# Three weight tiles of the first projection in two float32r parts, their low parts made on GpSimd

## The chip, the cores and the metric

The kernel runs on one core of one Trainium2 chip. The metric is the device time of one execution in microseconds (us). Engines are named as the profile names them: PE (TensorE matmul) with PEld (its weight loads), DVE (VectorE), ACT (ScalarE), POOL (GpSimd) and SP (SyncE, whose queue issues the transfers).

## What is computed

Two transformer-like blocks on 256 tokens of width 1024, in float32. Only the start of the first block bears on the change: one wide input projection, cut into parts, of which the first two feed a gated causal convolution 31 taps wide.

```python
h = x @ w_in[l] + b_in[l]
conv_a, conv_g, q, k, v, r, f_lr, gate_a, gate_b = jnp.split(h, split_points, axis=-1)
...
u = a * jax.nn.sigmoid(g)                       # a, g: conv_a, conv_g
u = conv(u, conv_w, width 31, causal, per channel) + conv_b
u = jax.nn.silu(layer_norm(u, ln_g, ln_b))
return u @ w_co + b_co
```

The rest of block 1 is a gated linear attention branch on `q, k, v, r, f_lr`, an output projection, a layer norm and a mixture of 64 experts; block 2 follows. The expert weights are most of the 527 MB that are read.

## The kernel before

Weights arrive as tiles of 128 x 2048 float32 (1 MB), one after the other in a fixed order, `W[0]`, `W[1]`, ...; the ring that holds them has four buffers. The first eight tiles are the projections `a` and `g` in turn: tile 0 is a0, tile 1 g0, tile 2 a1, tile 3 g1, tile 4 a2, tile 5 g2, tile 6 a3, tile 7 g3. Tiles 8 and 9 are `k`, then come `q`, `r`, `v`, the gates and the output projections. `proj_T` multiplies a tile in one of two ways:

- **Split.** `split` makes two float32r tiles: ACT casts the high part `hi` (L295; three buffers, `hlh`), DVE subtracts it from the weight for the low part `lo` (L297; two buffers, `hll`). PE then runs, for each half of the tile, 16 matmuls on `hi` (L343 with the high part of the input, L344 with its low part) and 8 on `lo` (L346): 48 per tile.
- **Whole.** With the tile's number in `WHOLE`, PE multiplies the float32 tile by the float32 input `xt` (L334), 16 matmuls per tile, each two records in the trace. ACT and DVE have nothing to do for it, and `xt` keeps a buffer of the weight ring until the last whole tile.

`proj_tok` (tiles 8, 9 and later) multiplies the other way round, with L362, L363 and L366 for the same three kinds.

Beside the projections run tasks that `pump` deals out at fixed places of the program. `fg` holds the decay of the attention branch (PE L490, then exponential and logarithm on ACT L492 and L495, then DVE L497, then PE L502, ...), `bg` the taps of the convolution. When a `g` tile is finished, `ev_g` computes sigmoid on ACT (L535) and the product `u` on DVE (L536, which reads PSUM), and queues 62 taps: two on ACT (L525), 60 on DVE (L527, `acc = u*w + acc`, all operands in SBUF). Four such groups make 240 taps on DVE. Behind the last tap DVE adds up the channels (L781), PE finishes that sum (L785), DVE subtracts the mean (L791) and adds up the squares (L794), PE finishes them (L799), and so on: the layer norm of the convolution, whose PE steps stand at fixed places between the projections of the later tiles. DVE also runs L692 (the scaled residual, `x1`) and L661 (a gate product) in that stretch.

A scheduler orders each engine's instructions when the program is built; on the chip each engine runs its own list in that order. The names of the change: `WHOLE`, `split`, `proj_T`, `nc.vector`, `nc.gpsimd`. POOL has nothing to do in the kernel before but a few powers on 1 to 8 columns (`rpow`, L379, and L1250).

Of the kernel before, what the change touches and what calls it, by code (L numbers as in the profile page):

```python
# [9 lines left out]
F32 = mybir.dt.float32  # L10
# [4 lines left out]
ALU = mybir.AluOpType  # L15
# [16 lines left out]
Z_MIN = 8  # L32
N_RING = (4, 1, 5)
E_BIAS, N_BIAS = 20, 7
WHOLE = (0, 5, 6, 7)

# [160 lines left out]
class Builder:  # L199
    def __init__(self, tc, I, ctx):  # L200
# [4 lines left out]
        self.after, self.ready, self.held = None, [], []  # L205
        self.whole = WHOLE
        pool = lambda **k: ctx.enter_context(tc.tile_pool(**k))
# [78 lines left out]
    def split(self, src, shape, pool, tag="hl"):  # L286
        nc = self.nc
        hi = self.t(pool, shape, tag + "h", F32R, bufs=3)
        lo = self.t(pool, shape, tag + "l", F32R, bufs=2)
        n = 2 if self.wi == 1 else 1  # L290
        late = lambda i: self.tc.issue_after(self.after[i].ins) if self.after is not None else ExitStack()
        for i in range(n):
            ks = slice(i * shape[1] // n, (i + 1) * shape[1] // n)
            with late(0):
                nc.scalar.copy(hi[:, ks], src[:, ks])  # L295
            with late(1):
                nc.vector.tensor_tensor(lo[:, ks], src[:, ks], hi[:, ks].bitcast(F32), ALU.subtract)  # L297
        self.pump(self.npump)
        return hi, lo

# [1432 lines left out]
```

## Time and profile before

| | |
|---|---|
| median of 3 runs | 1705.51 us (1702.78 to 1706.95) |
| the profiled execution, time | 1704.66 us |
| its span in the trace | 1702.9 us |
| PE busy / PEld busy | 87% / 68% |
| DVE busy / ACT busy / POOL busy | 44% / 31% / 1% |
| mean granted TensorE clock | 0.89 of full speed |

A share of the whole span says little here: the first 290 us (block 1 up to the experts) are matmuls with much DVE work, the next 850 us are the experts with the transfers at some 418 GB/s, and the rest is block 2. What the change touches lies between 30 and 70 us. A timeline row gives the start, the time from the first start to the last end of the merged instructions, engine, line, operation, output and inputs, shapes and the count; in brackets stands idle time just before it and what ended that. PE ends are modelled, so a tile's cost is best read from start to start.

### The profile page before, as it was taken

The page shows a single profiled execution, that of the slowest core. Times are in us where ns is not written, and L with a number is a line of the kernel's source. Part 1 is how long each engine was busy: PE and PEld are TensorE (multiplying, and loading weights), DVE is VectorE, ACT ScalarE, POOL GpSimd, SP SyncE. Part 2 cuts the span into 40 slices and gives each one's busy share as a digit, 9 for nine tenths or more (in the row PEclk, how much of TensorE's full clock was granted, in tenths as well). Part 3 has the DMA queues.
Part 4 walks back from the last instruction along what each step waited for, and adds up shares of the span by engine and source line. Part 5 has one row for each costly group of instructions (what it writes and reads, how often), then busy time and mean ns, then how long its engine had stood idle before and what let it go on. Part 6 is the DMA issues. An engine that isn't in the chain of part 4 may idle for free. (4 is left out here: it accounts for less than half of the span.)

```text
span 1702.9 us, 34326 instructions
## 1 busy us (share of the span) xinstructions
PE 1486.3 (87%) x14632; PEld 1154.9 (68%) x14632; DVE 749.8 (44%) x1487; ACT 527.4 (31%) x916; POOL 16.1 (1%) x22
## 2 busy tenths in 40 slices
PE   8999998877766787788888878868799999999998
PEld 7898996544444454455565545534699998899986
DVE  6999975311111121111121112211676866666645
ACT  4554552211111011111011111101585554555433
POOL 0000000000000000000000000000001000000000
PEclk9999999987788788887678788867899999999999
DMA  7555588999999999999999999999545444555551
GB/s 280 203 200 198 211 313 343 418 417 419 418 418 420 418 419 418 417 419 418 419 418 418 419 418 420 417 396 380 200 142 188 151 166 147 187 188 182 183 186 71
DMA packets 74516, 530.61 MB, mean 312 GB/s; under 512 B 8309, under 2 KB 8309, under 8 KB 11000
## 3 DMA queue, kind: packets, MB, share of 16 engines
q1 hardware_dynamic: 74354, 528.36, 78.1%
q8 instruction: 117, 1.92, 0.5%
q14 instruction: 39, 0.32, 0.1%
q10 hardware_dynamic: 6, 0.01, 0.0%
HBM read 527.29 MB, written 1.05 MB: 310 GB/s over the span
## 5 line engine op out<-in xcount | busy, mean ns | idle before, releaser
L966 PE MATMUL ps<-w,xg 128*32 128x256 f32 x4032 | 304.6, 449 | 74.0 <-DMA w<-in_wm_dram 71.6
L297 DVE TENSOR_TENSOR hll<-w,hlh 128x2048 fp32r<-128x2048 f32 (+1 forms) x112 | 252.5, 2256 | 96.3 <-PE ps L346 53.6
L966 PEld LDWEIGHTS ps<-w,xg 128*32 128x32 f32 x4032 | 131.6, 125 | 221.5 <-DMA w<-in_wm_dram 114.1
L295 ACT CAST hlh<-w 128x2048 fp32r<-128x2048 f32 (+1 forms) x112 | 210.6, 1881 | 164.0 <-PE ps L344 77.9
L343 PE MATMUL ps<-s,hlh 128*128 128x256 f32 x864 | 216.6, 289 | 1.0 <-ACT hlh L295 0.8
L344 PE MATMUL ps<-s,hlh 128*128 128x256 f32 x864 | 212.3, 283 | 0.3 <-DVE s L1284 0.2
L983 PE MATMUL ps<-w,hT 128*32 128x128 f32 x4032 | 167.9, 326 | 49.7 <-DMA w<-in_wm_dram 23.3
L972 DVE TENSOR_TENSOR h<-h,ps 64x256 f32<-64x256 f32 x63 | 26.6, 423 | 375.9 <-ACT h L971 375.9
L983 PEld LDWEIGHTS ps<-w,hT 128*32 128x32 f32 x4032 | 136.7, 131 | 69.5 <-DVE hT L977 23.7
L343 PEld LDWEIGHTS ps<-s,hlh 128*128 128x128 f32 x864 | 165.0, 191 | 4.5 <-issue 2.2
L344 PEld LDWEIGHTS ps<-s,hlh 128*128 128x128 f32 x864 | 165.5, 192 | 1.3 <-DVE s L318 0.6
L971 ACT ACTIVATE h<-ps 64x256 f32<-64x256 f32 x63 | 23.8, 378 | 406.1 <-PE ps L966 397.1
L987 DVE COPY ys<-ps 32x128 f32<-32x128 f32 x240 | 68.2, 284 | 155.4 <-PE ps L983 153.7
L987 ACT COPY ys<-ps 32x128 f32<-32x128 f32 x240 | 61.9, 258 | 236.3 <-PE ps L983 232.5
L346 PE MATMUL ps<-s,hll 128*128 128x256 f32 x864 | 121.3, 283 | 0.3 <-DVE hll L297 0.3
L346 PEld LDWEIGHTS ps<-s,hll 128*128 128x128 f32 x864 | 111.4, 192 | 0.5 <-DVE hll L297 0.5
L527 DVE SCALAR_TENSOR_TENSOR w<-w,vec,w 128x255 f32<-128x255 f32 (+14 forms) x240 | 94.3, 464 | 0.0
L1237 PEld LDWEIGHTS ps<-rel,con 32*128 32x128 f32 x512 | 82.2, 246 | 9.9 <-issue 7.6
L343 PE MATMUL ps<-w,hlh 128*128 128x256 f32 x352 | 86.1, 283 | 0.0
L1237 PE MATMUL ps<-rel,con 32*128 32x8 f32 x512 | 85.6, 298 | 0.0
L344 PE MATMUL ps<-w,hlh 128*128 128x256 f32 x352 | 84.8, 279 | 0.0
L995 PE MATMUL ps<-ys,WT 128*128 128x512 f32 x120 | 79.1, 816 | 0.0
(390 smaller groups left out, 1764.3 us busy)
## 6 DMA issues: line engine op xcount, KB each, us to landing
w<-in_wm_dram SPq DMA_DIRECT2D x378, 1024.0 KB, 19.8
w<-in_w_dram SPq DMA_DIRECT2D x115, 1024.0 KB, 4.8
gain<-in_row_dram SPq DMA_DIRECT2D x4, 512.0 KB, 5.0
w<-in_wpp_dram SPq DMA_DIRECT2D x2, 768.0 KB
w<-in_xT_dram SPq DMA_DIRECT2D x2, 512.0 KB, 5.5
w<-in_w_dram SPq DMA_DIRECT2D x2, 512.0 KB
x<-in_x_dram SPq DMA_DIRECT2D x1, 1024.0 KB
w<-in_wab_dram SPq DMA_DIRECT2D x1, 1024.0 KB, 5.3
```

The lines of the kernel that those rows point to most:

```text
L295: nc.scalar.copy(hi[:, ks], src[:, ks])
L297: nc.vector.tensor_tensor(lo[:, ks], src[:, ks], hi[:, ks].bitcast(F32), ALU.subtract)
L343: nc.tensor.matmul(o, hi[:, k, ms], xh[:, k, :], start=(k == 0), stop=False)
L344: nc.tensor.matmul(o, hi[:, k, ms], xl[:, k, :], start=False, stop=False)
L346: nc.tensor.matmul(o, lo[:, k, ms], xh[:, k, :], start=False, stop=(k == 7))
L527: nc.vector.scalar_tensor_tensor(a, u[:, m, :T - d], wj, a, ALU.mult, ALU.add)
L966: r = nc.tensor.matmul(pa[j * 32:(j + 1) * 32, :256], xg[:, k, c0:c0 + CAP], w[:, j * 256:(j + 1) * 256], start=(k == 0), stop=(k == KC - ...
L972: nc.vector.tensor_tensor(h, h, pa[64:128, :256], ALU.mult)
L983: r = nc.tensor.matmul(py[j % 2][j * 32:(j + 1) * 32, :P], hT[:, k % 2, k // 2, :], w[:, j * P:(j + 1) * P], start=(k == 0), stop=(k == 3) ...
L987: eng(ys[r0:r0 + CAP, c * 512 + j * P:c * 512 + (j + 1) * P], py[j % 2][j * 32:(j + 1) * 32, :P])
L995: self.nc.tensor.matmul(self.acc[t][c], WT[:rows, t * P:(t + 1) * P], ys[:rows, c * 512:(c + 1) * 512], start=False, stop=True, skip_group ...
L1237: nc.tensor.matmul(ps[:, i * 8:(i + 1) * 8], self.con[0:32, o + x:o + x + P], rel, start=True, stop=True)
```

## The change

Tiles 5, 6 and 7 (g2, a3, g3) leave `WHOLE` and go through `split` like their neighbours. In `split` the number `self.wi` has already been raised, so `POOLED = (6, 7, 8)` names the same three tiles; for them the subtraction that makes `lo` is issued on POOL. `self.whole` is empty in block 2, so nothing goes to POOL there.

```diff
-WHOLE = (0, 5, 6, 7)
+WHOLE = (0,)
+POOLED = (6, 7, 8)
...
             with late(1):
-                nc.vector.tensor_tensor(lo[:, ks], src[:, ks], hi[:, ks].bitcast(F32), ALU.subtract)
+                eng = nc.gpsimd if self.whole and self.wi in POOLED else nc.vector
+                eng.tensor_tensor(lo[:, ks], src[:, ks], hi[:, ks].bitcast(F32), ALU.subtract)
```

The scheduler's order changes with it. Line numbers of the changed kernel are one higher from L36 on and two higher behind the second hunk (L295 becomes L296, L297 L299, L527 L529, L781 L783, L794 L796).

POOL, from its first instruction of the program on. First the kernel before, then the changed one (`rs` and `crs` are outputs of powers):

```order
L379 ISA
L379 TENSOR_TENSOR rs_126_1320<-rp_1321,mhalf 128x4
L379 TENSOR_TENSOR rs_159_1584<-rp_1585,mhalf 128x4
L379 TENSOR_TENSOR crs_1985<-rp_1986,mhalf 128x1
L379 TENSOR_TENSOR crs_1990<-rp_1991,mhalf 128x1
```

```order
L299 ISA
L299 TENSOR_TENSOR hll_415<-w_412,hlh_414 128x2048
L299 TENSOR_TENSOR hll_483<-w_480,hlh_482 128x2048
L299 TENSOR_TENSOR hll_553<-w_550,hlh_552 128x2048
L381 TENSOR_TENSOR rs_132_1428<-rp_1429,mhalf 128x4
L381 TENSOR_TENSOR rs_165_1692<-rp_1693,mhalf 128x4
```

Three subtractions on 2048 columns, for tiles 5, 6 and 7, now stand ahead of the powers.

ACT, from the cast of tile 4 (`hlh_351` in both) up to the table of the logarithm; `e_344` is the sigmoid of tile 3, `e_439` and `e_475` that of tile 5, `ps_447` and its like the decay. Before, then changed:

```order
L295 CAST hlh_351<-w_349 128x2048
L535 ACTIVATE e_344<-ps_291,vec 128x256 x2
L525 ACTIVATE w_129<-w_128,vec 128x256 x2
L535 ACTIVATE e_439<-ps_412,vec 128x256 x2
L491 ACTIVATE w_126<-ps_447 128x512
L525 ACTIVATE w_129<-w_128,vec 128x256
L491 ACTIVATE w_126<-ps_450 128x512
L525 ACTIVATE w_129<-w_128,vec 128x256
L492 ACT_TABLE_LOAD
L492 ACTIVATE w_126<-w_126 128x1024
L295 CAST hlh_520<-w_518 128x2048
L495 ACT_TABLE_LOAD
```

```order
L296 CAST hlh_414<-w_412 128x2048
L296 CAST hlh_482<-w_480 128x2048
L537 ACTIVATE e_344<-ps_291,vec 128x256 x2
L527 ACTIVATE w_129<-w_128,vec 128x256 x2
L296 CAST hlh_552<-w_550 128x2048
L296 CAST hlh_628<-w_626 128x2048
L537 ACTIVATE e_475<-ps_422,vec 128x256 x2
L493 ACTIVATE w_126<-ps_486 128x512
L493 ACTIVATE w_126<-ps_489 128x512
L527 ACTIVATE w_129<-w_128,vec 128x256
L494 ACT_TABLE_LOAD
L494 ACTIVATE w_126<-w_126 128x1024
```

The casts of tiles 5 and 6 now stand ahead of the sigmoid of tile 3, and those of tiles 7 and 8 ahead of the sigmoid of tile 5.

DVE, around the last taps and the layer norm of the convolution (`hll` is the low part of a later tile, `x` the residual). Before, then changed:

```order
L527 SCALAR_TENSOR_TENSOR w_129<-w_128,vec,w_129 128x226
L692 SCALAR_TENSOR_TENSOR x_71<-x_71,gain 128x1024
L781 TENSOR_REDUCE e_1879<-w_129 128x256
L297 TENSOR_TENSOR hll_1885<-w_1882,hlh_1884 128x2048
L692 SCALAR_TENSOR_TENSOR x_71<-x_71,gain 128x1024
L297 TENSOR_TENSOR hll_1950<-w_1947,hlh_1949 128x2048
L791 TENSOR_TENSOR w_129<-w_129,mean_1877 128x1024 x2
L794 TENSOR_REDUCE e_1879<-w_1919 128x256
L794 TENSOR_REDUCE e_1880<-w_1919 128x256
L661 SCALAR_TENSOR_TENSOR w_1181<-w_1181,ps_1893 128x512
```

```order
L529 SCALAR_TENSOR_TENSOR w_129<-w_128,vec,w_129 128x226 x2
L299 TENSOR_TENSOR hll_1993<-w_1990,hlh_1992 128x2048
L783 TENSOR_REDUCE e_1987<-w_129 128x256
L299 TENSOR_TENSOR hll_2058<-w_2055,hlh_2057 128x2048
L793 TENSOR_TENSOR w_129<-w_129,mean_1985 128x1024 x2
L694 SCALAR_TENSOR_TENSOR x_71<-x_71,gain 128x1024
L796 TENSOR_REDUCE e_1987<-w_2027 128x256
L663 SCALAR_TENSOR_TENSOR w_1289<-w_1289,ps_2001 128x512
L796 TENSOR_REDUCE e_1988<-w_2027 128x256
```

Ahead of the second L794 stand the same low parts and all 240 taps in both; one L692 has gone behind it, and one L661 has come ahead of it. On PE the steps L785 and L799 stand between the same matmuls as before.

## Rows read from the trace of the kernel before

**Rows 1.** Windows of 10 us: busy us (count) per engine, PE clock, DMA share, GB/s
```profile
40.00:50.00 10.00, 10.00 (x48) 8.16 (x47) 10.00 (x27) 2.03 (x5) 0.00 (x0) 1.00 0.12 22
...
180.00:190.00 10.00, 10.00 (x87) 10.00 (x86) 10.00 (x11) 5.50 (x8) 0.00 (x0) 1.00 0.43 147
...
200.00:210.00 10.00, 8.10 (x53) 7.87 (x53) 8.10 (x11) 4.62 (x4) 1.07 (x2) 0.83 0.78 300
...
300.00:310.00 10.00, 8.61 (x194) 6.34 (x190) 5.84 (x27) 2.00 (x8) 0.00 (x0) 0.88 1.02 419
```

**Rows 2.** Timeline of PE around the whole tiles (columns told above)
```profile
35.16 0.28 PE L343 MATMUL ps<-w,hlh 128*128 128x256 f32 x1
...
40.81 7.07 PE L334 MATMUL ps<-w,w 128*128 128x256 f32 x32
47.71 1.88 PE L490 MATMUL ps<-gup,mean 128*128 128x512 f32 x4
49.43 13.98 PE L334 MATMUL ps<-w,w 128*128 128x256 f32 x64
```

**Rows 3.** Timeline of DVE, layer norm of the convolution
```profile
185.66 1.22 DVE L692 SCALAR_TENSOR_TENSOR x<-x,gain 128x1024 f32<-128x1024 f32 x1
186.79 3.86 DVE L781 TENSOR_REDUCE e<-w 128x256 f32<-128x2048 f32 x1
...
198.45 3.88 DVE L794 TENSOR_REDUCE e<-w 128x256 f32<-128x1024 f32 x2
202.24 0.68 DVE L661 SCALAR_TENSOR_TENSOR w<-w,ps 128x512 f32<-128x512 f32 x1
```

**Rows 4.** Timeline of PE, same stretch
```profile
190.79 0.67 PE L785 MATMUL ps<-e,ones 128*128 128x256 f32 x2 [0.27 <-DVE e L781]
...
202.38 0.83 PE L799 MATMUL ps<-ones,e 128*128 128x1 f32 x6 [1.46 <-DVE e L794]
```

**Rows 5.** Timeline of DVE from tile 4's low part to the decay
```profile
32.51 2.28 DVE L297 TENSOR_TENSOR hll<-w,hlh 128x2048 fp32r<-128x2048 f32 x1
35.86 0.87 DVE L536 SCALAR_TENSOR_TENSOR w<-ps,vec,e 128x256 f32<-128x256 f32 x2 [1.08 <-ACT e L535]
36.66 11.86 DVE L527 SCALAR_TENSOR_TENSOR w<-w,vec,w 128x248 f32<-128x248 f32 x31
...
57.39 1.29 DVE L497 SCALAR_TENSOR_TENSOR w<-ps,w 128x512 f32<-128x512 f32 x2
...
72.59 2.29 DVE L297 TENSOR_TENSOR hll<-w,hlh 128x2048 fp32r<-128x2048 f32 x1 [1.21 <-issue]
```

**Rows 6.** Timeline of ACT, same stretch
```profile
35.35 0.84 ACT L535 ACTIVATE e<-ps,vec 128x256 f32<-128x256 f32 x2 [4.82 <-PE ps L346]
...
47.97 0.84 ACT L535 ACTIVATE e<-ps,vec 128x256 f32<-128x256 f32 x2 [10.50 <-PE ps L334]
...
53.11 1.88 ACT L295 CAST hlh<-w 128x2048 fp32r<-128x2048 f32 x1
...
56.30 1.06 ACT L495 ACTIVATE w<-w 128x1024 f32<-128x1024 f32 x1
```

**Rows 7.** POOL's L379 at 1277 to 1281 us: duration ns min/median/max, first and last start
```profile
L379 POOL TENSOR_TENSOR krs<-rp,mhalf x2: 697/1720/2743, 1277.5 to 1280.2; 128x2 f32<-128x2 f32 x2
```

**Rows 8.** Timeline of DVE, same stretch
```profile
1277.41 2.28 DVE L297 TENSOR_TENSOR hll<-w,hlh 128x2048 fp32r<-128x2048 f32 x1
```

**Rows 9.** Timeline of POOL, a power beside taps and one on a column
```profile
149.47 1.18 POOL L379 TENSOR_TENSOR rs<-rp,mhalf 128x4 f32<-128x4 f32 x1 [149.01 <-DVE rp L378]
...
268.13 0.54 POOL L379 TENSOR_TENSOR rs<-rp,mhalf 128x1 f32<-128x1 f32 x1 [61.80 <-DVE rp L378]
```

**Rows 10.** Timeline of DVE: the taps beside it, and an operation on one column
```profile
16.47 0.15 DVE L1417 TENSOR_TENSOR gk<-vec 128x1 f32<-128x1 f32 x1
...
149.31 2.39 DVE L527 SCALAR_TENSOR_TENSOR w<-w,vec,w 128x248 f32<-128x248 f32 x6
151.62 2.28 DVE L297 TENSOR_TENSOR hll<-w,hlh 128x2048 fp32r<-128x2048 f32 x1
```

## The prediction

> **What bounds the kernel now.** I read the windows first, then the timelines of PE and DVE in block 1, then the few rows in which POOL and DVE work side by side. Between 40 and 50 us PE is busy all the time and so is DVE, at full clock, while transfers move next to nothing (22 GB/s); at 180 to 190 us PE and DVE are still both full [rows 1]. So two engines run level through the first 200 us of block 1, and the question is which of them sets its end. The answer stands at the layer norm of the convolution. PE reaches L785 with 0.27 us to wait for DVE, and at L799 it waits 1.46 us for DVE's L794 [rows 4]. DVE has no such wait: L692, L781 and L794 stand in a queue that is full from behind [rows 3], and the only idle time that its timeline shows between L536 at 35.86 us and this place is the 1.21 us ahead of one low part [rows 5]. DVE's queue sets when PE may pass L799; PE is the one that waits. From 300 us on the transfers are saturated (419 GB/s, DMA share 1.02) [rows 1]. They are issued as buffers of block 1 come free, and their total is fixed, so I take a shift of block 1's end as a shift of the end of the kernel, one to one.
>
> **The change, part by part.** *PE.* A split tile takes 5.65 us from start to start (35.16 to 40.81), a whole one 6.90 us (40.81 to 47.71; the two later ones 13.98 / 2 = 6.99) [rows 2]. Three tiles save 3 x 1.25 = 3.75 us of PE. That is the whole of what the change can give, and by itself it would end at 1704.66 - 3.75 = 1700.9 us. But it makes PE come 3.75 us earlier to a place where it already waits for DVE.
>
> *DVE, what it has to do.* DVE never made a low part for these tiles, so the change takes nothing from it. By the order, ahead of the second L794 stand the same taps and the same number of low parts; one L692 (186.79 - 185.66 = 1.13 us to the next start [rows 3]) has gone behind, one L661 (some 0.6 us; its record is 0.68 [rows 3]) has come ahead: -0.5 us.
>
> *ACT, three more casts.* Each takes 1.88 us [rows 6]. The cast of tile 6 now stands ahead of tile 3's sigmoid. With three buffers for the high part it must wait until PE has done tile 3, which is when the sigmoid started before, at 35.35 us [rows 6]; so the sigmoid starts at 37.23, and DVE's L536, 0.51 us behind it in the rows (35.86 - 35.35) [rows 5, 6], at 37.74. It is 1.88 us later, with one tap (11.86 / 31 = 0.383 us [rows 5]) done ahead of it: DVE loses 1.5 us. The cast of tile 8 stands ahead of tile 5's sigmoid in the same way; that starts at 40.81 + 5.65 + 1.88 + 0.26 = 48.6 us (0.26 is the step from 47.71 [rows 2] to 47.97 [rows 6]). DVE gets there with L536's 0.80 us (36.66 - 35.86) and 28 taps at 37.74 + 0.80 + 10.72 = 49.3 us, so nothing is lost there.
>
> *The decay.* ACT needs from the start of that sigmoid to the end of the logarithm 57.36 - 47.97 = 9.39 us, one cast of 1.88 us included [rows 6], which the new order puts elsewhere: 48.6 + 7.5 = 56.1 us. DVE, with L536 and 13 taps behind 49.3, stands at L497 at 55.0 and waits 1.1 us, where it came just in time before (57.39 [rows 5] behind 57.36). Against this, the idle 1.21 us of rows 5 goes, since PE frees that buffer earlier. Without any contact between POOL and DVE the sum is -0.5 + 1.5 + 1.1 - 1.2 = **+0.9 us**: DVE ends a little later than before and PE's 3.75 us become waiting at L785 and L799. What a longer wait there does to the clock is small: after the wait at L799 the window has 0.83 of full speed, a mean of the levels of 1.2 and 2.4 GHz [rows 1], and that loss is paid today too.
>
> *POOL, three subtractions of 2048 columns.* No row shows one. From below: the same operation on DVE, 2.28 us [rows 8]. From above: on a single column, where hardly anything but the fixed cost counts, a POOL power takes 0.54 us [rows 9] and a DVE operation 0.15 us [rows 10], a ratio of 3.6, which would make 8.2 us. One row shares the operation, the other the engine; I take the geometric middle, Q = 4.3 us, and keep both ends. The Trainium skill's page "GPSIMD Engine Reference", § 3.1, gives 4497 ns for a two-input operation of this size; by it the sum below would be 0.6 us larger. If nothing else happened Q would be free: each low part is needed only 16 matmuls (5.65 / 3 = 1.9 us) into its tile. For tile 5 POOL starts when PE is done with tile 3 (two buffers), 35.35, and has until 42.7 us; for tile 6 it starts at 41.0 and has until 50.1 (tile 6 starts behind L490 at 46.46 + 1.72, the step from 47.71 to 49.43 [rows 2]). The weight loads that now wait on SP for POOL's read are tiles 9 to 11, wanted only after 60 us, and transfers are idle there.
>
> *POOL against DVE.* This is the term that decides. At 1277.41 DVE runs a low part, with both inputs in SBUF [rows 8]; the POOL power that starts 0.1 us later takes 2.74 us, where the same power right behind it, beside no such operation, takes 0.70 [rows 7]. 2.74 - 0.70 = 2.04 us is what is left of DVE's 2.28 us: POOL waited until DVE was done. So the two share a way into SBUF and the later one is held out. In the other direction one place speaks for less: beside a power on 4 columns of 1.18 us [rows 9] DVE ran six taps in 151.62 - 149.31 = 2.31 us, 0.385 each [rows 10], no slower than the 0.383 of rows 5. That power got in between two taps, and reads 4 columns; how long it held the way the row cannot tell. A subtraction reads 2 x 2048 columns over its whole length. The Trainium skill, page "SBUF — State Buffer", § Who interferes with whom, says more than these rows: whichever starts first has the shared ports for its whole instruction, and a DVE instruction with two SBUF inputs is among those that contend. By that rule each Q below counts in full; by the taps of rows 10 alone it would count nothing, and the sum would stay at +0.9 us.
>
> I take it in full. Taps have both tensors in SBUF. Tile 5's subtraction (35.35 to 39.65) meets DVE only from 38.54 on, when L536, which reads PSUM, is done: Q - 3.2 us. Tile 6's (from 41.0) and tile 7's (from 46.6, when tile 5's buffer is free) fall into the 28 taps: Q each. Together 3Q - 3.2 = 9.7 us. The wait at L497 shrinks from 1.1 to some 0.5 us, since ACT's chain contains a tap that waits for the late L536. **Sum: -0.5 + 1.5 + 0.5 - 1.2 + 9.7 = +10.0 us**, and 1704.66 + 10.0 = 1714.7 us. The profiled execution lies 0.85 us below the median of the runs shown, so a median would be 1715.5; I say **1715**. With Q = 2.28 tile 5's part is nothing and the sum is +4.9 (1709.6); with Q = 8.2 it is +21.7 (1726.4). PE would stand at L502 for the late decay and at L785, always for DVE.
>
> **The rivals.** *No holding out in this direction* (rows 10 for it, rows 7 and 8 against): +0.9 us, 1705.6. This is the one on the other side, not slower: it decides if POOL lets taps through while it reads.
>
> *PE's gain arrives:* 1700.9. For it speaks that every low part before the layer norm is ready in time; against it that DVE has no idle time to give and the same work ahead of L794. It needs DVE to end 3.75 us earlier out of nothing, or L799 not to wait.
>
> *Taps keep POOL out* instead: back-to-back taps win each time. Tile 5's subtraction still costs 1.1 us, since it runs first. Tile 6's waits for the end of the 28 taps, 49.3, runs to 53.6, and PE, wanting it at 50.1, stands 3.5 us; of those 4.3 us 0.8 lie beside L536. Tile 7's takes the wait at L497 (1.1) and L497 itself (1.3, from PSUM) and costs 1.9. DVE: -0.5 + 1.5 - 1.2 + 1.1 + 3.5 + 1.9 = +6.3, 1711. Against it: in rows 9 a power got in between taps.
>
> **How the numbers follow.** Forecast, held out in full, 0.66; taps keep POOL out, or a half-way sharing, 0.13; no holding out 0.14; PE's gain arrives 0.07. A measurement of this kernel can tell 0.3%, 5.1 us. The forecast is beyond that but for its lowest end, the second case mostly (0.08 of 0.13); the other two are within it. Slower 0.73, same 0.25, faster 0.02, as even the whole gain of PE is under 5.1 us. The range reaches down to 1703.5, which takes in the case without holding out and leaves out PE's gain, and up to 1723, Q of 7.1; the rest up to 8.2 is left out with it.
>
> **What would show it.** Right: taps between 38 and 52 us with gaps or durations of some Q on DVE, beside three POOL rows; PE idle at L502 and for some us at L785; L794's end some 10 us later than 202.3. The steps before it: tiles 5 to 7 at 5.65 us on PE, L536 at 37.7. Wrong: taps at 0.383 us straight through POOL's rows and L794 at 203; or POOL rows of much more than 5 us with taps between, and PE idle at L346 of tile 6. If block 1 ends 10 us later and the kernel does not, the one-to-one step is wrong.

## The result, and the profile after

| | before | after |
|---|---|---|
| median (lowest to highest), 7 runs each | 1705.51 us (1702.78 to 1707.35) | 1713.28 us (1712.05 to 1716.79) |
| the profiled execution, its span | 1704.66, 1702.9 us | 1712.05, 1710.3 us |
| mean granted TensorE clock | 0.89 | 0.889 |

The ratio is 1.0051, with a 95% interval of 1.0041 to 1.0061: slower by 7 to 10 us, where 1715.0 us was forecast (+10). In the kernel after, code lines behind the change have moved: the cast is L296, the low part L299, the taps L529, the sigmoid and the product L537 and L538, the decay's exponential, logarithm, product and matmul L494, L497, L499 and L504, the layer norm of the convolution L783 (sum), L787 (PE), L796 (squares), L801 (PE).

The three new instructions are in the timeline of POOL, 34 to 66 us of the kernel after:

```profile
35.20 4.68 POOL L299 TENSOR_TENSOR hll<-w,hlh 128x2048 fp32r<-128x2048 f32 x1 [34.75 <-PE ps L348]
40.85 4.69 POOL L299 TENSOR_TENSOR hll<-w,hlh 128x2048 fp32r<-128x2048 f32 x1 [0.97 <-PE ps L348]
46.60 4.89 POOL L299 TENSOR_TENSOR hll<-w,hlh 128x2048 fp32r<-128x2048 f32 x1 [1.05 <-PE ps L348]
```

The timeline of DVE beside them (the same stretch; the row of 28 taps merges them):

```profile
36.61 0.88 DVE L538 SCALAR_TENSOR_TENSOR w<-ps,vec,e 128x256 f32<-128x256 f32 x2 [1.69 <-ACT e L537]
37.40 21.93 DVE L529 SCALAR_TENSOR_TENSOR w<-w,vec,w 128x248 f32<-128x248 f32 x28
59.25 0.87 DVE L538 SCALAR_TENSOR_TENSOR w<-ps,vec,e 128x256 f32<-128x256 f32 x2
...
65.62 1.29 DVE L499 SCALAR_TENSOR_TENSOR w<-ps,w 128x512 f32<-128x512 f32 x2 [0.70 <-ACT w L497]
```

In [rows 5] 31 taps took 11.86 us; here 28 take 21.93. Narrower windows of the same timeline single out where:

```profile
37.40 2.76 DVE L529 SCALAR_TENSOR_TENSOR w<-w,vec,w 128x248 f32<-128x248 f32 x1
...
40.47 5.35 DVE L529 SCALAR_TENSOR_TENSOR w<-w,vec,w 128x247 f32<-128x247 f32 x2
...
46.51 5.25 DVE L529 SCALAR_TENSOR_TENSOR w<-w,vec,w 128x245 f32<-128x245 f32 x2
```

One tap per subtraction is long, and all others keep their 0.46 us: the first by itself, the other two as the second of a pair (5.35 - 0.39 and 5.25 - 0.39 us). Each of the three starts or stands beside a row of POOL and ends 0.25 to 0.3 us behind that row's end (for the second: 40.47 + 5.35 = 45.82 against 40.85 + 4.69 = 45.54). The pair of products that reads PSUM, at 36.61, lies wholly inside POOL's first row and takes its usual 0.88 us.

What became of the delay is in the waits of PE up to 300 us (who waited for whom, total us, times, longest), and in two rows of PE's timeline:

```profile
PE ps L504 <- DVE w L499: 7.0, 1, 7.0
PE ps L787 <- DVE e L783: 5.9, 1, 5.9
...
66.37 3.66 PE L504 MATMUL ps<-w,con 128*128 128x512 f32 x4 [6.98 <-DVE w L499]
...
201.99 1.19 PE L787 MATMUL ps<-e,ones 128*128 128x256 f32 x2 [5.93 <-DVE e L783]
```

L785 of before waited 0.27 us [rows 4] and L502 not at all. DVE's squares, the last of which ended at 202.33 us before [rows 3], end here at 211.00 + 2.01 = 213.01 us, 10.7 us later (timeline of DVE):

```profile
198.26 3.59 DVE L783 TENSOR_REDUCE e<-w 128x256 f32<-128x2048 f32 x1
...
210.39 0.69 DVE L663 SCALAR_TENSOR_TENSOR w<-w,ps 128x512 f32<-128x512 f32 x1 [1.03 <-PE ps L348]
211.00 2.01 DVE L796 TENSOR_REDUCE e<-w 128x256 f32<-128x1024 f32 x1
```

Ahead of the last squares DVE waited 1.03 us for PE: the new order has put the gate product L663 there.

For the shifts below I use two landmarks of PE: the start of the router's bias matmul (L707 before, L709 after), the end of block 1's dense part, and the end of the last expert matmul (L966 before, L968 after):

```profile
242.17 1.16 PE L707 MATMUL ps<-wsm,vec 128*1 128x72 f32 x16
...
1187.91 1.07 PE L966 MATMUL ps<-w,xg 128*32 128x256 f32 x16 [0.94 <-SPq L1179]
```

```profile
252.59 1.16 PE L709 MATMUL ps<-wsm,vec 128*1 128x72 f32 x16
...
1196.78 1.07 PE L968 MATMUL ps<-w,xg 128*32 128x256 f32 x16 [0.20 <-SPq L1181]
```

The first fence is of before, the second of after. Block 1 ends 10.4 us later, the experts 8.9 us later, the program 7.4 us later by the profiled executions and about 8 by the medians. The last three figures differ by less than the executions of one kernel do (4.6 us among the seven of before).

### The profile page after: what moved, and what is told of

The parts are those of the page before. It is cut to its first block, busy times and chain, and to the rows that moved or that the text cites. A ratio compares the mean times of both kernels' runs of the same rounds, so it can differ in the third digit from the quotient of the medians.

```text
span 1710.3 us, 34445 instructions
## 1 busy us (share of the span) xinstructions
PE 1483.1 (87%) x14680; PEld 1150.9 (67%) x14680; DVE 760.9 (44%) x1487; ACT 532.9 (31%) x919; POOL 31.4 (2%) x25
## 5 line engine op out<-in xcount | busy, mean ns | idle before, releaser
L968 PE MATMUL ps<-w,xg 128*32 128x256 f32 x4032 | 306.8, 451 | 78.1 <-DMA w<-in_wm_dram 77.0
L299 DVE TENSOR_TENSOR hll<-w,hlh 128x2048 fp32r<-128x2048 f32 (+1 forms) x112 | 252.4, 2255 | 94.4 <-PE ps L348 53.5
L968 PEld LDWEIGHTS ps<-w,xg 128*32 128x32 f32 x4032 | 131.2, 125 | 228.2 <-DMA w<-in_wm_dram 123.1
L296 ACT CAST hlh<-w 128x2048 fp32r<-128x2048 f32 (+2 forms) x115 | 216.1, 1881 | 165.4 <-PE ps L346 88.1
L346 PE MATMUL ps<-s,hlh 128*128 128x256 f32 x864 | 212.2, 283 | 0.3 <-DVE s L1286 0.2
L346 PEld LDWEIGHTS ps<-s,hlh 128*128 128x128 f32 x864 | 165.5, 192 | 1.3 <-DVE s L320 0.5
L529 DVE SCALAR_TENSOR_TENSOR w<-w,vec,w 128x255 f32<-128x255 f32 (+14 forms) x240 | 105.5, 505 | 0.0
L345 PE MATMUL ps<-w,hlh 128*128 128x256 f32 x400 | 98.1, 284 | 0.0
L346 PE MATMUL ps<-w,hlh 128*128 128x256 f32 x400 | 96.4, 279 | 0.0
```

The costliest lines, as they stand in the source:

```text
L299: eng.tensor_tensor(lo[:, ks], src[:, ks], hi[:, ks].bitcast(F32), ALU.subtract)
L345: nc.tensor.matmul(o, hi[:, k, ms], xh[:, k, :], start=(k == 0), stop=False)
L346: nc.tensor.matmul(o, hi[:, k, ms], xl[:, k, :], start=False, stop=False)
L529: nc.vector.scalar_tensor_tensor(a, u[:, m, :T - d], wj, a, ALU.mult, ALU.add)
L968: r = nc.tensor.matmul(pa[j * 32:(j + 1) * 32, :256], xg[:, k, c0:c0 + CAP], w[:, j * 256:(j + 1) * 256], start=(k == 0), stop=(k == KC - ...
```

## The experiments

The shifts of the profiled executions against the profile of before, beside the ratio of the times:

| kernel | ratio to before, 95% interval | end of block 1 | end of experts |
|---|---|---|---|
| after | 1.0051 (1.0041 to 1.0061) | +10.4 us | +8.9 us |
| low parts on DVE | 1.0019 (1.0009 to 1.0028) | +5.5 | +3.8 |
| POOL only writes | 0.9981 (0.9971 to 0.9990) | -1.0 | -2.9 |
| each subtraction twice | 1.0126 (1.0109 to 1.0142) | +23.4 | +21.4 |
| tile 7 alone | 1.0055 (1.0039 to 1.0072) | +9.2 | +9.0 |
| tile 7 alone, second profile | one execution, 1715.78 us | +9.9 | +9.9 |
| tile 6 alone | 1.0019 (1.0009 to 1.0028) | +3.4 | +3.3 |
| tile 5 alone | 1.0037 (1.0025 to 1.0048) | +3.7 | +3.8 |
| tile 10 whole too | 0.9971 (0.9960 to 0.9982) | -1.9 | -3.6 |
| tiles 10 and 11 whole too | 1.0023 (1.0014 to 1.0033) | +1.6 | +1.8 |

A shift against this one profile of before is uncertain by about 0.9 us: two kernels that run the same program up to L490 (tile 10 whole too, tiles 10 and 11 whole too) reach it 0.8 and 0.9 us earlier than that profile does.

**The low parts on DVE.** POOL gets no subtraction; the tiles stay split. The scheduler orders DVE and ACT a little differently.

```diff
-POOLED = (6, 7, 8)
+POOLED = ()
```

> The changed kernel with the three low parts back on DVE (POOLED empty), so that only the two-part multiplication is left of the change. Theory (DVE's queue sets when PE may pass the layer norm of the convolution, POOL holds DVE out for its whole subtraction): DVE gets 3 x 2.2 us more work and loses nothing to POOL; with -1.1 us for the residual step that moves behind, +1.5 and +1.1 us of waiting on ACT and -1.2 us of old idle time the second L794 ends about 6.9 us later than before, some 4 us earlier than in the changed kernel: 1712. All taps take 0.38 us. Rival (PE sets the end, DVE has slack): PE's 3.75 us arrive, 1702.

No tap took over 0.49 us, the wait at L504 was gone, and PE waited at L787 alone, 11.9 us:

```profile
PE ps L787 <- DVE e L783: 11.9, 1, 11.9
```

Block 1 moved by +5.5 us, the time by 3 us (1708.12 us), some 4 us less than I expected. Three more subtractions of 2.28 us on DVE cost less than the same three on POOL, which are no work of DVE's at all.

**POOL only writes.** Each subtraction on POOL becomes a fill of the same tile.

```diff
-                eng = nc.gpsimd if self.whole and self.wi in POOLED else nc.vector
-                eng.tensor_tensor(lo[:, ks], src[:, ks], hi[:, ks].bitcast(F32), ALU.subtract)
+                if self.whole and self.wi in POOLED:
+                    nc.gpsimd.memset(lo[:, ks].bitcast(F32), 0.0)
+                else:
+                    nc.vector.tensor_tensor(lo[:, ks], src[:, ks], hi[:, ks].bitcast(F32), ALU.subtract)
```

> The changed kernel with POOL's three subtractions replaced by fills of the same tiles with zero: POOL writes 2048 columns, but reads nothing. The low parts of tiles 5 to 7 are left out of the product. PE, ACT and DVE have the same work in the same order. Theory (POOL's reading holds DVE's taps out): no tap is longer than 0.5 us, the second L794 ends 0.9 us later than before, 1706. Rival (any POOL instruction on a large tile holds DVE out): three taps are as long as the fills, and the end moves by their sum, 1708 to 1712. Rival (the casts and the new order cost the time, not POOL): as the changed kernel, 1713, with taps of 0.38 us.

POOL's and DVE's timelines of this kernel:

```profile
40.37 1.81 POOL L299 MEMSET hll<- 128x2048 f32 x1 [3.85 <-PE ps L350]
...
36.98 10.73 DVE L531 SCALAR_TENSOR_TENSOR w<-w,vec,w 128x248 f32<-128x248 f32 x28
```

The same 28 taps take 10.73 us, 0.383 each. Casts, order, buffers and PE's work are those of the changed kernel; what differs is how long POOL's instructions last and that they read nothing. Between this kernel and the changed one the 28 taps differ by 21.93 - 10.73 = 11.2 us, the end of block 1 by 10.4 + 1.0 = 11.4 us, and the time by 0.0070 x 1705 = 12 us. So the whole loss between the two is the held taps; the kernel without them was 0.2% faster than before. The Trainium skill ("SBUF — State Buffer", § Who interferes with whom) says that a DVE instruction with two SBUF inputs contends with a POOL instruction that reads SBUF and not with one that only writes it; these taps agree.

**POOL copies.** A one-input copy of the weight tile in place of the subtraction; as a difference to the kernel with the fill:

```diff
-                    nc.gpsimd.memset(lo[:, ks].bitcast(F32), 0.0)
+                    nc.gpsimd.tensor_copy(lo[:, ks], src[:, ks])
```

> The changed kernel with GpSimd copying the weight tile into the low part's place (one input read, the same bytes written) where it subtracted (two inputs read); the low parts of tiles 5 to 7 are thus another number, the work around them is the same. It tells whether it is reading that keeps the taps out or a two-input instruction of GpSimd. If reading alone does it: each copy holds one tap for its own length, about as long as the copy itself (an estimate between the fill's 1.81 us and the subtraction's 4.7 us, 2.5 to 3.5 us), three taps of 2 to 3.5 us, and block 1 ends 4 to 6 us later than before, time about 1708 to 1710 us. If only an instruction of GpSimd with two inputs does it: no tap over 0.55 us, and the time is that of the run in which GpSimd only wrote, 0.998 of the kernel before, about 1702 us.

With other numbers in the low parts the later stages compute something else: this program runs 64 matmuls of the experts more (4096 records instead of 4032), as do the two kernels with fewer taps, and ended 30 us later. So only block 1 is compared, here and there; it ended 2.9 us later than before, where 4 to 6 us were expected (1.4 of the 2.9 is an idle time of DVE that is told of under tile 6 alone). POOL's and DVE's timelines:

```profile
35.04 1.90 POOL L299 CAST hll<-w 128x2048 fp32r<-128x2048 f32 x1 [34.59 <-PE ps L350]
40.69 11.14 POOL L299 CAST hll<-w 128x2048 fp32r<-128x2048 f32 x2 [3.75 <-PE ps L350]
...
47.96 0.88 DVE L540 SCALAR_TENSOR_TENSOR w<-ps,vec,e 128x256 f32<-128x256 f32 x2
48.74 3.35 DVE L531 SCALAR_TENSOR_TENSOR w<-w,vec,w 128x234 f32<-128x234 f32 x2
```

A copy alone takes 1.90 us. The first was through before the taps began; the second and third held a tap each (3.35 us for two, where two take 0.84). So one input read is enough to hold a tap. But the second copy was itself kept out: its row and the third's, merged, last 11.14 us, where two copies take 3.8. That expectation was half right; the other half is the next question.

**Each subtraction twice.**

```diff
-                eng.tensor_tensor(lo[:, ks], src[:, ks], hi[:, ks].bitcast(F32), ALU.subtract)
+                for _ in range(2 if eng is nc.gpsimd else 1):
+                    eng.tensor_tensor(lo[:, ks], src[:, ks], hi[:, ks].bitcast(F32), ALU.subtract)
```

> The changed kernel with each of POOL's three subtractions done twice, one right behind the other, with the same result. Nothing else changes. Theory: each costs DVE its whole length again, 3 x 4.7 us: the second L794 ends some 14 us later than in the changed kernel, block 1 too, 1727; POOL is then full from 35 to 63 us, and DVE gets a tap in at most where one POOL instruction ends. Rival (POOL's length is hidden and the time goes elsewhere): 1713 or, where PE waits for the late low parts, up to 1718.

POOL's and DVE's timelines, and PE's waits:

```profile
34.96 28.61 POOL L300 TENSOR_TENSOR hll<-w,hlh 128x2048 fp32r<-128x2048 f32 x6 [34.51 <-PE ps L349]
...
37.15 27.07 DVE L530 SCALAR_TENSOR_TENSOR w<-w,vec,w 128x248 f32<-128x248 f32 x7
...
PE ps L349 <- POOL hll L300: 6.2, 3, 3.7
```

While POOL works without a pause, DVE gets one tap through for each of POOL's instructions: seven taps in 27 us. Block 1 ended 23.4 us later, as expected: the loss grows with POOL's reading time, nearly microsecond for microsecond (13.0 us more for some 14 us more on POOL).

**Tile 7 alone, and tile 7 alone once more.**

```diff
-WHOLE = (0,)
-POOLED = (6, 7, 8)
+WHOLE = (0, 5, 6)
+POOLED = (8,)
```

> Only tile 7 in two parts, its low part on POOL; tiles 5 and 6 whole as before. The order of ACT's casts ahead of the sigmoids is then that of before. Theory: one tap held out for some 4.6 us, 0.6 us for the gate product that comes ahead, -1.2 us of old idle time: the second L794 ends some 4 us later than before, 1709. If the three costs of the changed kernel were not alike (the first of them smaller, since DVE waits or reads PSUM at that time) one tile costs more than a third of it. Rival (a cost per kernel, not per subtraction): 1713. Rival (PE's gain counts): 1704.

> The kernel with tile 7 alone once more, unchanged, for a second profile of it. In the first its subtraction on GpSimd (alone about 4.7 us) was kept out by some 17 taps that followed one another without a gap, and lasted 10.93 us; in the changed kernel the second and third subtraction got in after one tap; and a small power of GpSimd (128x4) lasted 1.16 to 1.19 us beside taps in five kernels and 4.90 to 4.94 us beside the same taps in three others. If which engine gets the ports is settled by where the program puts the two instructions (the same in each execution, give or take nanoseconds), this profile shows 10 to 11.5 us again. If it falls out anew in each execution, it shows 4.7 to 5.1 us with one tap held for about as long in some of them, and the time is then 3 to 6 us less than 1714 us. The first run's times, 1713.27 to 1714.38 us in four executions, speak for the first; I hold it at 75 in 100.

The first expectation missed: one subtraction cost nearly as much as three (1713.99 us). POOL's, DVE's and ACT's timelines of the first run, then its load queue on SP:

```profile
41.22 10.93 POOL L299 TENSOR_TENSOR hll<-w,hlh 128x2048 fp32r<-128x2048 f32 x1 [40.76 <-ACT hlh L296]
...
39.67 8.00 DVE L529 SCALAR_TENSOR_TENSOR w<-w,vec,w 128x243 f32<-128x243 f32 x21
47.64 0.88 DVE L538 SCALAR_TENSOR_TENSOR w<-ps,vec,e 128x256 f32<-128x256 f32 x2
48.43 3.97 DVE L529 SCALAR_TENSOR_TENSOR w<-w,vec,w 128x233 f32<-128x233 f32 x1
...
57.16 1.91 ACT L296 CAST hlh<-w 128x2048 fp32r<-128x2048 f32 x1 [7.66 <-DMA w<-in_w_dram]
59.08 1.28 ACT L494 ACT_TABLE_LOAD   x1
...
52.17 10.05 SPq L267 DMA_DIRECT2D w<-in_w_dram  x4
```

Here the taps kept POOL out. They ran at 0.381 us each (8.00 / 21) as if POOL were not there, and POOL came in when DVE turned to the two products with a PSUM input: it ended at 52.15, 4.5 us behind their start, and held the one tap that followed them. That is the rival "taps keep POOL out". Its price lies elsewhere than I had put it: not in PE waiting for the low part, but in the weight tile that POOL had not yet read, a wait that the prediction put at nothing. The load into that buffer went out at 52.17 us, the next cast on ACT waited for it until 57.16, and the decay's exponential and logarithm stand behind that cast; L504 on PE started at 66.37 us, after 5.06 us of waiting, as late as in the changed kernel. The second profile of the same kernel showed the same:

```profile
41.80 11.17 POOL L299 TENSOR_TENSOR hll<-w,hlh 128x2048 fp32r<-128x2048 f32 x1 [41.35 <-ACT hlh L296]
```

So it does not fall out anew each time (one execution of 1715.78 us).

**Tile 6 alone, tile 5 alone.**

```diff
-WHOLE = (0,)
-POOLED = (6, 7, 8)
+WHOLE = (0, 5, 7)
+POOLED = (7,)
```

> The change for tile 6 alone; tiles 5 and 7 stay whole float32, as before. It is to tell why GpSimd's one subtraction for tile 7 lay 10.93 us in the run with tile 7 alone (from 41.22 to 52.15 us of its trace), where it took 4.69 and 4.89 us amid the same taps in the changed kernel. Theory A (the engine that asks second gets the ports after the instruction that runs, whatever follows; the long one had another cause): the subtraction takes 4.7 to 5.1 us, one tap is held for about 4.9 us, the scan's reduction ends some 4 us later than before, and the time is about 1708 us. Theory B (a run of VectorE instructions with two SBUF inputs, each ready when the one ahead ends, keeps GpSimd out until VectorE comes to an instruction with a PSUM input or to a gap; in the changed kernel GpSimd got in because each of its subtractions followed the one ahead, which had begun while VectorE was idle): the subtraction begins by the profile at about 40 us, amid taps, lasts until some 5 us after the next pair of products with a PSUM input or the next gap (47.6 us in the run with tile 7 alone), so 8 to 13 us in all; PE then waits at the decay's matmul and at the statistics' matmul by 3 to 6 us each, and the time is about 1713 us. I hold B at 60 in 100.

```diff
-WHOLE = (0,)
-POOLED = (6, 7, 8)
+WHOLE = (0, 6, 7)
+POOLED = (6,)
```

> The change for tile 5 alone; tiles 6 and 7 stay whole float32, as before. In the changed kernel the first of GpSimd's subtractions began at 35.20 us while VectorE had nothing to do, lay beside two products with a PSUM input that ran at their usual 0.48 us, and held one tap for 2.76 us. By both theories of the run with tile 6 alone it begins at once here, takes 4.7 us and holds one tap for about 2.8 us (2.4 us more than a tap). That is all that VectorE loses: block 1 should end 2 to 3 us later than before less what the split tile's 1.25 us on PE wins where VectorE has slack, and the time is 1706 to 1709 us. If VectorE's loss is not what moves block 1, and the split tile's gain on PE counts, it is 1704 us or less.

The first of these could not decide its question: the order put the subtraction of tile 6 ahead of the taps (POOL at 36.69 for 4.68 us, the PSUM products at 37.15), so POOL was in before any tap came, as with tile 5 (34.49 for 4.67 us). Both give the price of one held tap: the first three taps took 4.47 and 4.52 us together, where three take 1.2, so 3.3 us were lost, and block 1 ended 3.4 and 3.7 us later, though a split tile saves PE 1.25 us. The end of block 1 is not the price of the tap alone. DVE also stood idle for 1.46 and 1.45 us, where before it did not wait (timeline of DVE, tile 6 alone):

```profile
159.26 0.69 DVE L320 TENSOR_TENSOR m<-e,m 128x512 fp32r<-128x512 f32 x1 [1.46 <-ACT m L320]
```

ACT was late there because it had waited for a POOL power of 4.93 us, which took 1.18 us before (last section). The runs with tile 7 alone have the same idle time. For tile 5 I had expected 2.4 us of loss; DVE came to its products 1.7 us earlier than in the changed kernel, so more of POOL's row lay beside the tap.

**Fewer taps.** 128 of DVE's 240 taps left out, in the kernel before and in the changed one.

```diff
-                self.bg += [lambda m=m, k=k: tap(m, k) for k in reversed(range(CW)) for m in (2 * j, 2 * j + 1)]
+                self.bg += [lambda m=m, k=k: tap(m, k) for k in reversed(range(CW // 2 + 1, CW)) for m in (2 * j, 2 * j + 1)]
```

> The kernel before with 128 of the 240 taps on DVE left out (the convolution keeps 15 of its 31 taps). DVE has some 49 us less to do in block 1. It is the base for the next one. Theory: DVE has idle time and PE does not wait at L785 or L799, so block 1 ends 2 to 4 us earlier than before (its waits there and the slow clock behind them): 1702. Rival (DVE has slack already): as before, 1705.

> The changed kernel with the same 128 taps left out. Theory: DVE is still held out by POOL for some 4.6 us a time, but has the time; PE's 3.75 us arrive: 3.75 us less than the same cut of the kernel before, 1698. Rival (what POOL takes from DVE counts wherever DVE stands): some 8 us more than the same cut of the kernel before, 1710.

Their times, 1729.40 and 1735.44 us, are not to be compared with the kernel before, only with each other. The first went as expected in block 1 (-4.7 us, 0.9 of it ahead of L490; no wait left at L785 and L799). The second missed: with DVE's queue relieved, PE's saving of 3.75 us should have come through, but the changed kernel still ended block 1 5.9 us later than the other (+1.2 against -4.7), a little less than the 8 us of the rival. Its timelines of PE and ACT:

```profile
66.52 3.59 PE L504 MATMUL ps<-w,con 128*128 128x512 f32 x4 [7.20 <-DVE w L499]
...
59.91 0.60 ACT L527 ACTIVATE w<-w,vec 128x256 f32<-128x256 f32 x1 [10.86 <-DVE w L538]
```

The end of L504 is 5.9 us later than in the kernel before with fewer taps, and so are the two landmarks behind it, L787 and L709: all of the delay arises there. ACT's queue has a tap of its own (L527) ahead of the decay's exponential, that tap needs the product L538, and L538 stands behind the 28 taps. So the held taps reach the end by two ways, DVE's queue and PE standing at L504, and 5.9 us would stay if DVE had time to spare later.

**More whole tiles.** If DVE's queue sets the end of block 1, the opposite change should help: the kernel before with tile 10, or 10 and 11, multiplied whole, so with one or two low parts fewer on DVE.

```diff
-WHOLE = (0, 5, 6, 7)
+WHOLE = (0, 5, 6, 7, 10)
```

> The kernel before with one more whole tile, tile 10 (the first of q): the other way round from the change. PE gets 1.25 us more, DVE 2.2 us less, ACT a cast less. Theory (DVE's queue sets the end at L794, PE waits there for 0.27 and 1.9 us): the second L794 ends 2.2 us earlier, PE comes 1.25 us later and the two meet; PE passes L799 about 1.2 us earlier than before and saves what the slow clock behind the wait costs, up to 2 us: 1702 to 1704. Rival (PE sets the end): 1.25 us later, 1707. The input tile keeps a buffer of the weight ring for 12 us more; if a load comes late by that, PE waits for a transfer at tiles 8 to 11.

```diff
-WHOLE = (0, 5, 6, 7)
+WHOLE = (0, 5, 6, 7, 10, 11)
```

> The kernel before with tiles 10 and 11 whole float32 too, so with two of VectorE's subtractions of 2.28 us fewer in block 1 and 2.5 us more on PE; the run with tile 10 alone ended block 1 1.9 us earlier and took 0.9971 of the time before. If VectorE's queue is still what the end of block 1 hangs on, the second tile gains about as much again: 0.995 to 0.996, about 1698 us. If PE is the bound once tile 10 is whole (the waits for the statistics were gone from its trace), the second tile costs its 1.25 us on PE: 0.9975 to 0.999, about 1702 to 1703 us. I hold the second at 70 in 100.

The one tile gave 1701.46 us, 0.9971 (0.9960 to 0.9982), faster than both kernels of this case. PE's steps of the layer norm, L785 and L799, wait for DVE no more (timeline of PE; [rows 4] had 1.46 us at L799):

```profile
201.16 0.95 PE L799 MATMUL ps<-ones,e 128*128 128x1 f32 x8
```

Of the 4.5 us that the medians differ by, block 1 shows 1.9, and 0.8 of those lie ahead of L490, where the programs are the same; the experts show 1.8 more (next section). With the second tile the gain was gone (1708.64 us), and by more than the 1.25 us of PE that I had put against it. PE had a new wait, 2.2 us for ACT's scaling of the attention output, which waited for a POOL power that lasted 4.13 us (last section). The two make up the 3.5 us by which block 1 ends later than with one tile (+1.6 against -1.9): all that is added to PE arrives. With one more whole tile PE and DVE are level; beyond it PE is the bound.

## Why the prediction was right, point by point

- **PE saves 3.75 us and it does not arrive: right.** A split tile takes 5.65 us again, and the saving went into the waits at L504 and L787, both for DVE, both named.
- **The order, the casts, the decay: +0.9 us forecast without any contact (+0.3 in the sum, with the shorter wait at L497), -0.7 us measured** at the last squares of the kernel in which POOL only writes (-1.0 at the end of block 1). The cast of tile 6 came earlier than I had put it, and L538 at 36.61 us instead of 37.74. The step that failed is the one that lets the cast wait until the sigmoid's old place, 35.35 us: the cast was released by the last matmul on tile 3's high part (L346, before the change L344), ahead of the eight on its low part that the sigmoid waits for (timeline of ACT, changed kernel). The size of the miss is near what the shifts can tell.

```profile
34.16 1.91 ACT L296 CAST hlh<-w 128x2048 fp32r<-128x2048 f32 x1 [2.07 <-PE ps L346]
```

- **Q: 4.3 us forecast, 4.68, 4.69 and 4.89 us measured.** The 4497 ns that the Trainium skill gives ("GPSIMD Engine Reference", § 3.1) was nearer than my geometric middle, and all three rows are still 4 to 9% above it.
- **POOL holds the taps out: right, by 11.2 us instead of 9.7.** Three taps of 2.76, 4.96 and 4.86 us, and no other tap longer than usual. Less the 0.46 us of a free tap, the second and third lost 4.5 and 4.4 us where I had 4.3; for tile 5 I had 1.1 us where 2.3 were lost, since L538 was through 1.1 us earlier.
- **DVE's end: +10.0 us forecast, +10.7 measured**. The taps were put 1.5 us too small, the order and the casts 1.0 to 1.6 us too large, and the 1.03 us in which DVE waits for PE at L663 were not in the sum. That it came out within 0.7 us is in part luck.
- **The rule of one instruction each.** In the changed kernel the rule that whichever starts first has the shared ports for its whole instruction (the Trainium skill, "SBUF — State Buffer", § SBUF: two separate sides) describes the rows: the tap waits for POOL's whole instruction. It does not say who comes next when one side is a row of instructions without a gap, and there the rival with 0.13 was not wrong but true of another program: with tile 7 alone the taps kept POOL out, by measurement.
- **One to one to the end: mis-sized.** 10.4 us at the end of block 1 became 8.9 us at the end of the experts and about 8 in the medians. I took the transfers' total as fixed and their start as given by block 1. But the changed kernel has more of them done when the experts begin. Windows of the 24 us ahead of the first expert matmul, before and then after (the last number is GB/s):

```profile
257.30:281.30 24.00, 22.02 (x119) 17.16 (x118) 13.21 (x55) 7.06 (x12) 1.08 (x2) 1.00 0.80 312
```

```profile
267.80:291.80 24.00, 22.00 (x119) 17.17 (x117) 13.16 (x55) 7.05 (x12) 1.08 (x2) 1.00 0.89 355
```

43 GB/s over 24 us are 1.03 MB, one expert tile, which at the 419 GB/s of [rows 1] is 2.5 us. The seventeenth of the expert loads goes out 18.4 us ahead of the first expert matmul, where before it went out 10.6 us ahead. In both SP issues it as soon as a matmul of PE (L366, now L368) is done, and in the changed kernel that is an earlier one; what in the order makes it so is not shown. The table above sorts by this. In the four other kernels whose load goes out 18.3 us ahead (low parts on DVE, POOL only writes, each subtraction twice, tile 10 whole) the experts also end 1.6 to 2.0 us better than block 1; in the four where it goes out 10.6 or 11.1 us ahead (tiles 5, 6 and 7 alone, tiles 10 and 11) the two ends agree within 0.2 us. No run moved that one load by itself, so this is a strong pattern and not an experiment on it.

## What to carry to other kernels

Before work goes to POOL, look at what DVE runs beside it: where that is a queue of instructions with two SBUF inputs, a POOL instruction that reads a whole tile from SBUF takes up to its own length out of DVE (2.3 to 4.5 us of 4.7 here), or is kept waiting itself, and here three of them cost more than the same work on DVE (+10.4 against +5.5 us of block 1). Ask also what stands behind the instruction that is kept waiting on either engine: the buffer it still reads, the load into that buffer, and the queue of the engine that wants the load. And when one engine waits for another at a join, work taken off the waiting engine is worth nothing; here one tile moved the other way, from DVE to PE, was worth 0.3%, of which block 1 shows less than half.

## What the runs showed of the hardware that I had not expected

**Who gets in is not settled by who asks first alone.** Amid a run of taps, POOL's second and third subtraction in the changed kernel and five of the six in the doubled one held the very next tap or the one after. With tile 7 alone (twice) and in the second copy, POOL waited out 17 to 19 taps and came in at the first DVE instruction with a PSUM input. In the first group a held tap lay at most three taps back, in the second the taps had run freely since they began. The moment at which POOL came does not tell them apart: the next tap started less than 0.01 and 0.30 us after POOL's row where POOL got in (changed kernel), and 0.08, 0.20 and 0.36 us after it where it did not. A small power shows both outcomes without a held tap near it. Beside six taps it lasted 1.18 us before [rows 9, 10]; with tile 6 alone, again beside taps and a low part, 4.93 us. POOL's and DVE's timelines there:

```profile
149.65 4.93 POOL L381 TENSOR_TENSOR rs<-rp,mhalf 128x4 f32<-128x4 f32 x1 [108.28 <-DVE rp L380]
...
149.49 2.02 DVE L529 SCALAR_TENSOR_TENSOR w<-w,vec,w 128x250 f32<-128x250 f32 x5
151.43 2.28 DVE L299 TENSOR_TENSOR hll<-w,hlh 128x2048 fp32r<-128x2048 f32 x1
153.63 1.65 DVE L603 SCALAR_TENSOR_TENSOR w<-w,dec,ps 128x256 f32<-128x256 f32 x4
```

Again it ends (154.58) just behind the first DVE instructions with a PSUM input (153.63). It was 4.90 us with tile 10 whole, 4.94 with tile 5 or tile 7 alone, 4.95 with the copies, and 1.16 to 1.19 us in the changed kernel, with the low parts on DVE, with the fills and with each subtraction twice. With tiles 10 and 11 whole it was the next power that lasted 4.13 us. The long power has a price: in all six profiles with 4.90 to 4.95 us DVE then stood idle for 1.44 to 1.49 us at L318 (now L320), which waits for ACT, and in the kernel before and the four with 1.16 to 1.19 us it did not. What tells the two outcomes apart stays open; a kernel that leaves a power or a subtraction on POOL beside such a stream has either of two times for it, 3.7 us apart here.

**A matmul behind a wait.** L502's four matmuls took 1.88 us before and take 3.66 us as L504 (1.32 and 2.79 us to the next matmul's start), behind 6.98 us in which PE had nothing to do. The granted clock in windows of 6 us, from 63 us before and from 66 us after, is 1.00 and 0.69, between the levels of 2.4 and 1.2 GHz:

```profile
63.00:69.00 6.00, 6.00 (x30) 4.45 (x30) 6.00 (x11) 5.94 (x8) 0.00 (x0) 1.00 0.63 222
```

```profile
66.00:72.00 6.00, 5.63 (x14) 3.23 (x15) 6.00 (x11) 5.95 (x6) 0.00 (x0) 0.69 0.30 82
```

I had weighed the clock only at L799. In the changed kernel this loss ended in the wait at L787, where DVE was later still; in the kernel with fewer taps, which had no such wait, it is part of the 5.9 us.
